# A two-layer decoder trunk on one core: window values as a difference, input weights kept split, early products by operand half, and running sums on GpSimd

## The chip, the core and the metric

The kernel runs on one core of a Trainium2 chip. The core has TensorE for matrix products (PE in the profile, with its weight loads as PEld), VectorE (DVE), ScalarE (ACT), GpSimd (POOL) and SyncE (SP), which issues most of the DMAs. The metric is the device time of one execution in microseconds. Before the change three runs took 1911.7 us (median), 1904.19 us and 2302.37 us.

## The reference

The input is x of 1024 positions by 1024 channels, in 32-bit floats. There are two layers, and each has two sub-layers, with an RMS norm before and after each, and with shift, scale and gate made from a vector c by a product with `ada_w`.

```python
h = rms_norm(x, g_pre_mix[l]) * (1.0 + scale_m) + shift_m
proj = h @ w_in[l] + b_in[l]                       # 1024 -> 512 q, 128 k, 128 v, 512 u
q, k = partial_rotary(q), partial_rotary(k)        # first 16 of 64 dims of each head
attn_out = sliding_window_attention_with_sinks(q, k, v, sinks[l])   # 8 heads, 2 kv heads, window 128
pool_out = causal_pool_mixer(u, pool_w[l], pool_scale[l])           # means over 2, 4, 8, 16 positions
mix = concat([attn_out, pool_out]) @ w_out[l]
x = x + gate_m * rms_norm(mix, g_post_mix[l])
h = rms_norm(x, g_pre_ffn[l]) * (1.0 + scale_f) + shift_f
f = (silu(h @ w_gate[l]) * (h @ w_up[l])) @ w_down[l]               # 1024 -> 2816 -> 1024
x = x + gate_f * rms_norm(f, g_post_ffn[l])
```

With blocks of 128 positions, a query at place i of its block sees the keys at places j > i of the block before, and the keys at j <= i of its own block. In the first block there are only its own keys. The softmax also has one sink logit per head. The pooling mixer takes, for each of four groups of 128 channels, the mean over the last 2, 4, 8 or 16 positions, subtracts the token itself, and maps the group by a 128x128 matrix.

## The kernel before

Every large product is made from operands that are split in two: `hi` is the operand rounded to TensorE's 32-bit matmul format, `lo` is the rest, and `mm3` (L268 in the profile) adds three products, hi by hi, hi by lo and lo by hi. `split` makes the two parts: an ACT copy (L220) and a DVE subtraction (L221). So each weight tile that comes from memory costs one DMA, one ACT and one DVE instruction before TensorE can use it. `weight` loads and splits one tile (512 columns); `one_ahead` hands it out and asks for the next one, so that one tile is prepared ahead.

The positions are worked on in two halves (h = 0 and 1) of 512, each in four tiles t of 128. In a layer the mixing stage comes first, and then the channel-mixing stage, which is a dense run of products. The mixing stage goes as follows.

- `q_pass`, `kv_pass` and `u_pass` project a half: for each of 8 slices k of the channels (4 double slices in `kv_pass`) they take a weight tile and make 12 products of 512 columns (256 in `kv_pass`). Each weight of `w_in` is thus loaded and split twice in a layer, once for each half.
- `attention(h)` gives 8 groups, one for each tile t and each kv head n. A group makes transposed keys and queries, scores (`att_scores`, one 128x128 score tile a head, in which the places j > i hold the scores with the block before and the others those with its own block), the softmax, transposed probabilities (`att_probs`), and the product with the values (`att_values`, into the bank `pv`). Before the change `att_probs` made two masked copies by four GpSimd selects: `here`, with j <= i (L1048), and then `seen` masked in place to j > i (L1053). `here` met the block's own values and `seen` those of the block before.
- `pool_mix(h)` gives four steps, one for each window width. A width w needs log2(w) running sums over 527 columns or fewer (L1145, on DVE), a scaled subtraction (L1149), a split, and one `mm3`, which is issued one step late.
- `mix_out(h)` multiplies the concatenated result by `w_out` in `natural_proj`: two halves nh of the output columns, each in four banks of PSUM, first with the pooled channels (4 slices), then with the attention's. Ahead of the first attention slice it calls `finish_off(last)`, which issues whatever of the half's attention is left.
- While half 1 is mixed, half 0 goes on: `post_norm` (L695, sums of squares L596, a chain of short instructions L327 to L334), `normalise` (L636 on DVE, L638 on ACT), eight transposed pieces (`pre_norm_piece`, ACT L649), and then `up_firsts`: early products of the channel-mixing stage for three column pairs p and two halves kh of the depth. kh = 0 needs pieces 0 to 3, and kh = 1 needs pieces 4 to 7.

TensorE's order in this part is written by hand. `weave(main, *sides)` walks through the dense work (`main`), and each side chain becomes due after a number of columns has been issued. A gap is given in STEPs of 12 x 512 columns, that is 12 products. `LEADS` holds the gaps inside an attention group, `attention`'s last argument is the gap between groups, and the numbers in `yield` are those of the other chains. The other engines' orders follow from the order of the program and a scheduler. Each engine works through its own queue in order, and so does SP with the DMAs.

## Time and profile before

| what | value |
|---|---|
| median of 3 runs | 1911.7 us |
| the profiled execution's own time | 1908.17 us |
| its span, first to last instruction | 1906.5 us |
| TensorE busy | 1852.5 us, 97% of the span |
| VectorE busy | 1522.5 us, 80% |
| ScalarE busy | 938.1 us, 49% |
| GpSimd busy | 128.9 us, 7% |
| mean granted TensorE clock | 0.993 |
| DMA | 341.81 MB, mean 179 GB/s |

The mixing stage of layer 0 lies between about 30 and 275 us of the span, and that of layer 1 between about 955 and 1215 us. In between, and after, lie the channel-mixing stages. A TensorE instruction's duration in the profile is longer than the time from its start to the next start, since products overlap; the time to the next start is what a product costs. A stretch in which an engine waits is shown in square brackets with what ended it. PEclk is the share of full clock that TensorE was granted.

### The profile page before, as it was taken

How to read it: one execution, taken by the hardware profiler on the slowest of the kernel's cores; microseconds unless marked ns; L12 is line 12 of the kernel's file. 1: busy time of each engine (PE TensorE's matmuls, PEld its weight loads, DVE VectorE, ACT ScalarE, POOL GpSimd, SP SyncE). 2: the span in 40 equal slices, each digit the busy share in tenths (PEclk: the TensorE clock that was granted, in tenths of full speed). 3: DMA queues.
4: the chain of work that ended last, by engine and by line, in shares of the span. 5: the costliest groups of instructions: out<-in, count | busy, mean ns of one | idle time of the engine just before them, and what ended most of it. 6: DMA issues, size and time to landing. Idle time of an engine off the chain costs nothing. (4 is left out here: it accounts for less than half of the span.)

```text
span 1906.5 us, 25287 instructions
## 1 busy us (share of the span) xinstructions
PE 1852.5 (97%) x8662; PEld 1519.9 (80%) x8662; DVE 1522.5 (80%) x2507; ACT 938.1 (49%) x1775; POOL 128.9 (7%) x226
## 2 busy tenths in 40 slices
PE   7999989999999999999999998999999999999998
PEld 5877778888878788888887876788888887888886
DVE  7898876678898888788868988756878888867687
ACT  4775686663222223445558757855622222234452
POOL 0022122000000000000001312210000000000000
PEclk9999999999999999999999999999999999999999
DMA  9346554555555665944553573446654565574343
GB/s 333 124 135 182 187 160 144 188 172 188 199 176 190 209 204 167 325 150 149 172 180 93 166 228 122 139 149 204 216 190 148 199 214 195 193 254 159 116 138 116
DMA packets 229536, 341.81 MB, mean 179 GB/s; under 512 B 17016, under 2 KB 126472, under 8 KB 229408
## 3 DMA queue, kind: packets, MB, share of 16 engines
q1 hardware_dynamic: 228800, 338.10, 54.0%
q10 hardware_dynamic: 576, 2.10, 0.3%
q8 instruction: 68, 1.11, 0.2%
q14 instruction: 60, 0.49, 0.1%
q0 software_dynamic: 32, 0.00, 0.0%
HBM read 267.25 MB, written 72.89 MB: 178 GB/s over the span
## 5 line engine op out<-in xcount | busy, mean ns | idle before, releaser
L220 ACT ACTIVATE hi<-raw 128x1024 fp32r<-128x1024 f32 (+1 forms) x388 | 332.9, 869 | 404.1 <-PE acc L268 255.4
L221 DVE TENSOR_TENSOR lo<-raw,hi 128x1024 fp32r<-128x1024 f32 (+1 forms) x388 | 385.1, 999 | 117.8 <-ACT hi L220 113.3
L268 PE MATMUL acc<-t,hi 128*128 128x512 f32 x1408 | 432.3, 390 | 2.4 <-ACT hi L220 2.3
L268 PEld LDWEIGHTS acc<-t,hi 128*128 128x128 f32 x1408 | 263.8, 188 | 58.8 <-ACT hi L220 4.8
L268 PE MATMUL acc<-hT,hi 128*128 128x512 f32 x960 | 304.9, 399 | 4.7 <-ACT hi L220 3.0
L268 PE MATMUL acc<-t,lo 128*128 128x512 f32 x704 | 272.3, 390 | 1.0 <-DVE lo L221 1.0
L268 PEld LDWEIGHTS acc<-hT,hi 128*128 128x128 f32 x960 | 175.1, 190 | 38.9 <-ACT hi L220 3.9
L268 PE MATMUL acc<-bh,hi 128*128 128x512 f32 x520 | 203.0, 390 | 0.0
L268 PE MATMUL acc<-bh,lo 128*128 128x512 f32 x520 | 202.6, 390 | 0.0
L268 PE MATMUL acc<-hT,lo 128*128 128x512 f32 x480 | 189.2, 394 | 0.0
L1313 DVE TENSOR_TENSOR fn<-acc,fn 128x512 f32<-128x512 f32 x220 | 150.4, 684 | 38.8 <-PE acc L268 38.6
L268 PEld LDWEIGHTS acc<-t,lo 128*128 128x128 f32 x704 | 132.2, 188 | 30.4 <-DVE lo L221 3.0
L268 PE MATMUL acc<-ph,hi 128*128 128x512 f32 x328 | 126.6, 390 | 0.0
L268 PE MATMUL acc<-hi,hT 128*128 128x512 f32 (+1 forms) x448 | 123.4, 348 | 1.0 <-ACT hT L220 1.0
L1240 ACT ACTIVATE fn<-fn 128x512 f32<-128x512 f32 x44 | 27.8, 633 | 181.2 <-DVE fn L1313 181.2
L268 PEld LDWEIGHTS acc<-bh,lo 128*128 128x128 f32 x520 | 97.7, 188 | 20.3
L268 PEld LDWEIGHTS acc<-bh,hi 128*128 128x128 f32 x520 | 97.7, 188 | 20.0
L268 PE MATMUL acc<-b,hi 128*128 128x512 f32 x352 | 108.4, 389 | 0.0
L268 PEld LDWEIGHTS acc<-hT,lo 128*128 128x128 f32 x480 | 91.0, 190 | 20.5 <-DVE lo L221 0.9
L268 PE MATMUL acc<-hi 128*128 128x512 f32 x256 | 102.8, 402 | 3.9 <-ACT hi L220 2.8
L268 PE MATMUL acc<-lo,hi 128*128 128x512 f32 x256 | 101.3, 396 | 0.1
L220 ACT ACTIVATE bh<-two_b 128x512 fp32r<-128x512 f32 x100 | 62.3, 623 | 71.4 <-PE acc L268 70.7
(304 smaller groups left out, 3238.8 us busy)
## 6 DMA issues: line engine op xcount, KB each, us to landing
raw<-in_w_gate_dram SPq DMA_DIRECT2D x44, 512.0 KB
raw<-in_w_up_dram SPq DMA_DIRECT2D x44, 512.0 KB
raw<-in_w_in_dram SPq DMA_DIRECT2D x80, 256.0 KB
cfb<-in_ada_w_dram SPq DMA_DIRECT2D x80, 256.0 KB
raw<-keeps SPq DMA_DIRECT2D x40, 512.0 KB
keeps<-fn SPq DMA_DIRECT2D x66, 256.0 KB
ar<-in_ada_w_dram SPq DMA_DIRECT2D x64, 256.0 KB
two_b<-in_w_down_dram SPq DMA_DIRECT2D x30, 512.0 KB
```

The costliest lines, as they stand in the source:

```text
L220: a = nc.scalar.activation(hi, src, AF.Copy)
L221: v = nc.vector.tensor_sub(lo, src, hi.bitcast(F32))
L268: return nc.tensor.matmul(dst, lhs, rhs, start=start, stop=stop)
L1240: nc.scalar.activation(g, g, AF.Silu)
L1313: nc.vector.tensor_add(halves_of(dst)[m], bank, halves_of(src)[m])
```

## The change

Four things are changed, together with numbers that set TensorE's order.

1. **Values with a difference.** `seen` is no longer masked. All probabilities of a tile, masked by nothing, meet the values of the block before, and the copy `here` (j <= i) meets the difference of the block's own values and those of the block before. The sum is the same. Two of the four selects of a group go, and for the first block both. The difference is made by GpSimd (`tensor_sub`, 128x128, once a tile) and split by ACT and DVE into new tiles `dz`. The product with the unmasked probabilities comes first, and the one with `here` after a gap of its own.
2. **Weights stored split.** `weight_once` writes the two parts of a tile to memory (two DMAs of 256 KB) when it is first made, and loads both by one DMA of 512 KB when it is next needed. This is done for all weights `u` and, in layer 1, also for `q` and `kv`: 28 tiles.
3. **Early products in another order.** For the first three column pairs `up_firsts` makes kh = 0 of all pairs first, and then kh = 1 of all; pieces 4 to 7 are so needed 16 groups of three products later.
4. **Running sums on GpSimd** in `pool_mix` (now L1152).

Besides, `natural_proj` of half 1 takes two of its four banks for nh = 1 from another pool of banks, the score rows are 192 columns apart instead of 129, and `one_ahead` can prepare two tiles ahead (for `u` of half 1). The core of the diff:

```diff
+    def weight_once(key, *srcs):
+        if key in parted:
+            both = part("lo", 1024)
+            nc.sync.dma_start(both.bitcast(F32), parted.pop(key))
+            return both[:, 0:512], both[:, 512:1024]
+        hi, lo = weight(*srcs)
+        if key[0] == "u" or key[-1] == "1":
+            parted[key] = both = dr.tile([P, 1024], F32, tag=key, name="parted", bufs=1)
+            for i, src in enumerate((hi, lo)):
+                nc.sync.dma_start(both[:, i * 512 : (i + 1) * 512], src.bitcast(F32))
+        return hi, lo
...
-            banks = [acc_bank() for _ in range(NT)]
+            spare = 2 if nh and free else 0
+            banks = [msc_bank() for _ in range(spare)] + [acc_bank() for _ in range(spare, NT)]
...
-        for v in views:
-            nc.gpsimd.affine_select(
-                out=v, in_=v, pattern=[[0, GRP], [-1, P]], compare_op=ALU.is_gt,
-                fill=0.0, base=0, channel_multiplier=1,
-            )
...
+            if n == 0:
+                if blk:
+                    nc.gpsimd.tensor_sub(step, qkvs[t][:, QK:QKV], attn["raw"])
+                attn["raw"] = qkvs[t][:, QK:QKV]
...
-            yield LEADS[4]
-            att_values(blk, n, probs, cat, t)
+                used = [attn["v"], att_vals("dz", step)] if blk else []
+                attn["v"] = att_vals("vz", qkvs[t][:, QK:QKV])
+                attn["vals", blk] = used or [attn["v"]]
+            parts = list(zip(attn["vals", blk], probs))
+            for i, (vals, prob) in enumerate(parts):
+                yield LEADS[4 + i]
+                att_values(n, vals, prob, n + i == 0, n == NKV - 1 and i == len(parts) - 1, cat, t)
-    LEADS = (0.8, 0.8, 0.25, 3.2, 2.2)
+    LEADS = (0.9, 0.85, 0.21, 2.72, 1.2, 0.94)
...
-                nc.vector.tensor_add(nxt[:, lo:n], cur[:, lo:n], cur[:, lo - width : n - width])
+                nc.gpsimd.tensor_add(nxt[:, lo:n], cur[:, lo:n], cur[:, lo - width : n - width])
...
-            yield 2.0 if h else 3.0
+            yield 1.7 if h else 2.82
...
-        jobs = [(p, kh) for p in pairs for kh in range(2)]
+        jobs = [(p, kh) for kh in range(2) for p in pairs] if room else [(p, kh) for p in pairs for kh in range(2)]
...
-        att = attention(0, qkvs[0], par["sink"], cats[0][0], 0.5, 3.8)
+        att = attention(0, qkvs[0], par["sink"], cats[0][0], 0.47, 3.23)
...
-        att = attention(1, qkvs[1], par["sink"], cats[1][0], 14.0, 4.2)
+        att = attention(1, qkvs[1], par["sink"], cats[1][0], 14.0, 3.95)
...
-                yield 0.5
+                yield GAPS[k // HK]
...
-        ask1 = one_ahead(all_rows(u_rows, l))
+        ask1 = one_ahead(all_rows(u_rows, l), 2)
...
-                if i == 2 * HK - 1:
+                if i == 2 * HK * FIRST[0] - 1:
```

Three places show what moves. The first is TensorE's queue in layer 0, where the last attention group of half 0 ends inside `mix_out(0)`. `msc<-ident,sb` are the transposes of the probabilities, `pv<-pth,vz` and `pv<-pth,dz` the products with values and with their difference, `acc<-...` those of `mix_out`; `uT` and `pt` are the low parts of its left operand, `pt` from the first attention slice on. Before:

```order
L273 MATMUL msc<-ident,sb 128x128 x4
L268 MATMUL acc<-hi 128x512
L268 MATMUL acc<-lo,hi 128x512
L268 MATMUL acc<-hi,uT 128x512
L268 MATMUL acc<-hi 128x512
L268 MATMUL acc<-lo,hi 128x512
L268 MATMUL acc<-hi,uT 128x512
L268 MATMUL acc<-hi 128x512
L268 MATMUL acc<-lo,hi 128x512
L268 MATMUL acc<-hi,uT 128x512
L268 MATMUL pv<-pth,vz 128x512 x6
L268 MATMUL acc<-hi 128x512
```

With the change the last group's transposes stand in front of `mix_out(0)`, 31 rows ahead of its last product:

```order
L285 MATMUL acc<-hi 128x512
L285 MATMUL acc<-lo,hi 128x512
L285 MATMUL acc<-hi,uT 128x512
L285 MATMUL pv<-pth,dz 128x512 x3
L285 MATMUL acc<-hi 128x512
L285 MATMUL acc<-lo,hi 128x512
L285 MATMUL acc<-hi,uT 128x512
```

The last value products stood 9 products behind the transposes, right ahead of the first attention slice; now they stand further from the transposes, and products of pooled slices (`uT`) follow them.

The second place is POOL's queue in layer 0 while half 1 is pooled. `pth<-pth` are the selects on the probabilities, `pt<-uT` the first and `pt<-pt` the further running sums of a width, `sb<-qkv` the difference of the values. Before:

```order
L1048 AFFINE_SELECT pth<-pth 128x512 x2
L1053 AFFINE_SELECT pth<-pth 128x512 x2
L931 CAST vz<-vz_zero 128x64 x2
L1098 COPY sb<-sk 128x4
L1048 AFFINE_SELECT pth<-pth 128x512 x2
```

And with the change:

```order
L1059 AFFINE_SELECT pth<-pth 128x512 x2
L948 CAST vz<-picks 128x64 x2
L1152 TENSOR_TENSOR pt<-pt 128x525
L1152 TENSOR_TENSOR pt<-pt 128x521
L948 CAST dz<-picks 128x64 x2
L1152 TENSOR_TENSOR pt<-uT 128x527
L1152 TENSOR_TENSOR pt<-pt 128x525
L1098 TENSOR_TENSOR sb<-qkv 128x128
L1152 TENSOR_TENSOR pt<-pt 128x521
L1101 COPY sb<-sk 128x4
L1152 TENSOR_TENSOR pt<-pt 128x513
L1059 AFFINE_SELECT pth<-pth 128x512 x2
```

Six running sums (the last two of width 8 and all four of width 16) now stand between the selects of two neighbouring attention groups.

The third place is SP's queue in layer 0 at the start of `u_pass` of half 0. `raw<-in_w_in_dram` are loads of weight tiles, `cfa<-in_ada_w_dram` loads for the gate, `parted` the stores of split weights. Before:

```order
L233 DMA raw<-in_w_in_dram 128x512 x2
L551 DMA cfa<-in_ada_w_dram 128x512 x4
L233 DMA raw<-in_w_in_dram 128x512 x3
L522 DMA ar<-in_ada_b_dram 1x512
L523 DMA ar<-in_g_post_mix_dram 1x512
```

And with the change:

```order
L236 DMA raw<-in_w_in_dram 128x512 x2
L568 DMA cfa<-in_ada_w_dram 128x512 x4
L253 DMA parted<-hi 128x512
L253 DMA parted<-lo 128x512
L253 DMA parted<-hi 128x512
L253 DMA parted<-lo 128x512
L236 DMA raw<-in_w_in_dram 128x512 x3
L539 DMA ar<-in_ada_b_dram 1x512
L540 DMA ar<-in_g_post_mix_dram 1x512
```

The loads of the next three tiles now stand behind the stores of two tiles, and a store waits until its tile is split.

More of the change, by code (lines that the diff above doesn't have):

```diff
@@ L97, in hybrid_decoder_kernel @@
     dr = ctx.enter_context(tc.tile_pool(name="dr", bufs=1, space=DRAM))
-    SMALL = dict(junk=1, st=9, rs=8, ss=4, halo=8, rows=1, cols=2, colp=4, sk=2)
+    const.tile([P, 32], F32, name="fill")
+    ident_r = const.tile([P, P], F32R, name="ident")
+    const.tile([P, 56], F32, name="fill2")
+    SMALL = dict(junk=1, st=9, rs=8, ss=4, halo=4, cols=2, colp=4, sk=2)
     SHARED = dict(hT=8, fn=4, raw=2, hi=3, lo=3, sa=2, sb=2, ar=2, ada=1, ph=3, G=1)
     REGIONS = dict(
-        mix=dict(cfa=2, cfb=2, qkv=5, bqkv=1, uT=4, pt=2, vz=5, qT=1, pth=4, pwh=1, pwl=1),
+        mix=dict(cfa=2, cfb=2, qkv=5, bqkv=1, uT=4, pt=2, vz=4, dz=2, qT=1, pth=4, pwh=1, pwl=1),
         up=dict(t2=8, t1=8, t3=8, b22=8, t4=8),
@@ L243, in after, with one_ahead @@
         )
-    def one_ahead(makers):
+    def one_ahead(makers, ahead=1):
         makers = iter(makers)
-        held = [next(makers)()]
+        held = [make() for _, make in zip(range(ahead), makers)]
         def ask():
-            now_ = held.pop()
             for make in makers:
@@ L254, in ask @@
                 break
-            return now_
+            return held.pop(0)
         return ask
@@ L757, in finish, with natural_proj @@
             nc.sync.dma_start(out[0, h * T + rows.start : h * T + rows.stop, cs], fn[t][:, cs])
-    def natural_proj(fn, left, wsrc, ss, G, last):
+    def natural_proj(fn, left, wsrc, ss, G, last, free):
         K = len(left)
@@ L803, in drain @@
             pass
-    vz_zero = const.tile([P, HD], F32, name="vz_zero")
-    nc.vector.memset(vz_zero, 0.0)
     halos = {}
@@ L1160, in pool_mix, with mix_out @@
             late = (g, hi, lo_)
[L1161 removed]
+            yield 1.7 if h else 2.82
         mapped(*late)
[L1164 removed]
+    def mix_out(l, cats, G, last, free=False):
         order = [*range(GRP, KD), *range(GRP)]
@@ L1179, in mix_out @@
         ss = t_("ss", [P, 8])
-        return fn, ss, natural_proj(fn, left, wsrc, ss, G, last)
+        return fn, ss, natural_proj(fn, left, wsrc, ss, G, last, free)
     HK = KD // 2
@@ L1255, in operand @@
             return hi, lo
-        nxt = operand(*jobs[0])
+        nxt, xs_ = operand(*jobs[0]), []
         yield
@@ L1630, in gate_flow @@
             one, two = ada_gate(l, 0)
-            yield from ada_flow([one], [cats[0][1][:, i, :] for i in range(4)], 1.8)
+            yield from ada_flow([one], [cats[0][1][:, i, :] for i in range(4)], 2.25)
             while 1 not in cats:
                 yield 0.5
-            yield from ada_flow([two], [cats[1][1][:, i, :] for i in range(4)], 1.8)
+            yield from ada_flow([two], [cats[1][1][:, i, :] for i in range(4)], 1.91)
         gate = Chain(gate_flow())
-        att = attention(0, qkvs[0], par["sink"], cats[0][0], 0.5, 3.8)
+        att = attention(0, qkvs[0], par["sink"], cats[0][0], 0.47, 3.23)
         def dense():
```

89 lines of the change are left out of this document (39 added, 50 removed).

## The prediction

> **What bounds the kernel now.** I read the page first, then busy time by stretches, then who TensorE waited for in the stretches where it idles, and last the order of instructions around those waits. The page says that TensorE is the bound:
>
> ```profile
> span 1906.5 us, 25287 instructions
> ...
> PE 1852.5 (97%) x8662; PEld 1519.9 (80%) x8662; DVE 1522.5 (80%) x2507; ACT 938.1 (49%) x1775; POOL 128.9 (7%) x226
> ```
>
> The change leaves the number of products as it is: a group of attention has six value products before and after, the early products only change places. So what can be won is TensorE's idle time and its slow clock. The view by stretches shows where these lie. After the stretch and its length come busy us and instruction counts of PE, PEld, DVE, ACT and POOL, then the granted clock, DMA share and GB/s.
>
> ```profile
> 30.00:160.00 130.00, 127.39 (x749) 108.59 (x749) 114.91 (x245) 93.81 (x231) 24.86 (x49) 1.00 0.51 165
> 160.00:176.00 16.00, 13.25 (x48) 9.20 (x47) 14.65 (x27) 6.57 (x16) 5.45 (x7) 0.91 0.67 208
> 176.00:225.00 49.00, 47.92 (x221) 37.28 (x220) 41.92 (x88) 30.64 (x80) 3.19 (x6) 1.00 0.65 207
> 225.00:275.00 50.00, 42.02 (x222) 33.79 (x221) 39.11 (x77) 42.73 (x95) 15.17 (x22) 0.97 0.49 158
> 275.00:955.00 680.00, 677.36 (x3050) 558.87 (x3050) 543.32 (x765) 292.47 (x458) 14.60 (x21) 1.00 0.57 187
> 955.00:1098.00 143.00, 140.58 (x791) 119.79 (x790) 119.40 (x253) 97.68 (x240) 25.76 (x52) 1.00 0.47 147
> 1098.00:1112.00 14.00, 11.53 (x40) 7.73 (x40) 12.39 (x22) 4.73 (x9) 5.13 (x7) 0.88 0.65 194
> 1112.00:1160.00 48.00, 46.81 (x218) 36.30 (x217) 41.17 (x86) 30.08 (x78) 3.18 (x6) 1.00 0.63 205
> 1160.00:1215.00 55.00, 47.51 (x234) 38.39 (x233) 40.54 (x79) 44.89 (x100) 15.73 (x26) 0.91 0.44 148
> 1215.00:1300.00 85.00, 84.47 (x393) 69.38 (x392) 52.47 (x93) 51.86 (x111) 12.77 (x17) 1.00 0.42 134
> 1300.00:1850.00 550.00, 548.73 (x2434) 453.03 (x2433) 440.09 (x607) 213.81 (x301) 0.00 (x0) 1.00 0.56 186
> ```
>
> The two long dense stretches idle 2.6 us of 680 and 1.3 us of 550, and the change barely touches them. The nine others are the mixing stages. Length less busy PE gives 2.6, 2.8, 1.1, 8.0, 2.4, 2.5, 1.2, 7.5 and 0.5 us, 28.5 us together. The clock (1 less PEclk, times length) adds 1.4, 1.5, 1.7 and 5.0 us in the four stretches below 1.00, 9.6 us. So about 38 us can be won at most, 2.0% of the span. Three parts: the running of attention beside the projections (30 to 160, 955 to 1098; call it A, 5.0 us), the end of the first half's attention (160 to 176, 1098 to 1112; B, 5.2 us idle and 3.1 of clock), and the second half's start (225 to 275, 1160 to 1215; C, 15.5 us idle and 6.5 of clock). The rest is 2.8 us. PE's waits in B of layer 0 and in C of layer 0 (engine, line, waited for: total us, times, longest):
>
> ```profile
> PE acc L268 <- ACT hi L220: 1.4, 1, 1.4
> PE pv L268 <- POOL pth L1048: 0.9, 2, 0.6
> PE pv L268 <- POOL pth L1053: 0.5, 2, 0.3
> ...
> PE msc L273 <- DVE fn L636: 2.2, 2, 2.0
> PE msc L273 <- DVE hi L970: 2.0, 1, 2.0
> PE acc L268 <- ACT hi L220: 1.5, 1, 1.5
> PE msc L273 <- ACT raw L649: 1.2, 1, 1.2
> PE msc L268 <- ACT qT L982: 0.9, 1, 0.9
> ```
>
> One product's price, 225.03 / 991 = 0.227 us, and so 2.72 us for a STEP of 12, comes from the chain of waits:
>
> ```profile
> 1611.47 225.03 PE acc L268 x991
> ```
>
> **The change part by part.** *End of attention (B).* The four selects of the last group stand between transposes and value products, and nothing covers them, since only 9 products (2.0 us) lie between; then `mix_out` waits 1.4 us for the cast of the finished output. With the change the groups start every 3.23 STEPs instead of 3.8: 7 x 0.57 x 2.72 = 10.9 us earlier for the last of eight, and the leads inside a group are 7.25 - 6.82 = 0.43 STEP shorter, 1.2 us more. The queue in front of this text shows the same: the last products leave before the attention slices come. If the earlier place holds, all of B goes, 8.3 us. What would uncover it again is a group that runs 5 us late.
>
> *Stored weights.* Each of 28 second uses loses a cast and a subtraction:
>
> ```profile
> L220 ACT ACTIVATE hi<-raw 128x512 fp32r<-128x512 f32 x167 | 103.5, 628 | 122.4 <-PE acc L268 83.7 <-issue 22.0 <-DMA raw<-in_w_in_dram 12.6
> L221 DVE TENSOR_TENSOR lo<-raw,hi 128x512 fp32r<-128x512 f32 x167 | 118.3, 716 | 51.9 <-ACT hi L220 47.6 <-DMA raw<-in_w_gate_dram 2.1 <-DMA raw<-keeps 1.8
> ```
>
> That is 17.6 us of ACT and 20.0 us of DVE. Only the 16 `u` tiles lie in C. There the wait for ACT's cast (L220, 1.5 us a layer, 3.0 for two) goes, since that cast is no longer made. The price lies in half 0: SP's stores wait for the split of a tile prepared one step ahead, and three loads are queued behind. Three loads issued from 40.03 on fed a cast at 43.92:
>
> ```profile
> 40.03 1.76 SPq L233 DMA_DIRECT2D raw<-in_w_in_dram  x3
> ...
> 43.92 0.62 ACT L220 ACTIVATE hi<-raw 128x512 fp32r<-128x512 f32 x1
> ```
>
> so the path from one tile's split to the next batch's is 0.63 + 0.72 + 3.9 + 0.63 + 0.72 = 6.6 us, and with 0.3 us for a store's issue 6.9 us, against two steps of about 3.2 us (12 products and the transposes of a piece): 0.5 us late, twice a pass, in two layers: 2 us. Bounds: nothing, if the tiles are split earlier; 2.5 us each time, 10 us, if each cast and subtraction waits behind a wide one (1.06 and 1.22 us in the rows below).
>
> *Early products by half.* Pieces 4 to 7 were forced one behind the other; PE then waited for L649 (1.2 us, in layer 1 0.8). Now they have 16 groups of three products, 16 x 0.68 = 10.9 us, and gaps of 1.06 STEP. I count all 2.0 us. The silu of three pairs also moves behind all kh = 0 jobs; nothing on PE's path is credited for that.
>
> *Running sums.* DVE loses 16, 12, 8 and 4 sums of about 0.7 us, 29 us in all. What a sum costs on GpSimd no row shows. The nearest are its selects, which read one operand:
>
> ```profile
> L1053 POOL TENSOR_SCALAR_AFFINE_SELECT pth<-pth 128x512 fp32r<-128x512 f32 x56 | 47.1, 864 | 0.0
> L1048 POOL TENSOR_SCALAR_AFFINE_SELECT pth<-pth 128x512 fp32r<-128x512 f32 x56 | 41.4, 739 | 43.2 <-ACT pth L220 34.9 <-DVE pth L221 6.3 <-DVE rs L332 1.4
> L1098 POOL COPY sb<-sk 128x4 f32<-128x4 f32 x32 | 15.6, 486 | 283.6 <-PE msc L273 203.8 <-DVE cfb L636 28.8 <-ACT hi L969 16.7
> L931 POOL CAST vz<-vz_zero 128x64 fp32r<-128x64 f32 x32 | 9.9, 329 | 666.4 <-DVE fn L636 627.4 <-PE pv L268 39.1
> ...
> L934 DVE TENSOR_TENSOR vz<-qkv,vz 128x128 fp32r<-128x128 f32 x16 | 4.8, 298 | 1.5 <-PE pv L268 1.5
> L1145 DVE TENSOR_TENSOR pt<-uT 128x527 f32<-128x527 f32 x16 | 12.0, 748 | 3.7 <-ACT uT L901 2.6 <-POOL pth L1053 0.6
> ```
>
> A sum reads two operands: between 0.74 us (one select) and 1.73 us (two of the slower). I take 1.3 us. The Trainium skill (GPSIMD Engine Reference, Performance versus the Vector engine) gives 4497 ns for an add of 2048 columns, by which 527 would take an estimated 1.16 us; it also says that such work belongs on VectorE, which speaks against this part of the change. No run here shows it yet.
>
> In the tightest place six sums stand between the selects of two groups: 6 x 1.3 = 7.8 us, two selects 1.7, and two copies, four casts and a difference about 2.7 us, 12.2 us against a group's period of 3.95 x 2.72 = 10.7 us. From the transposes to the masked product there are 2.14 STEPs, 5.8 us, of which a cast, a subtraction and two selects take 3.0; the 2.8 us left cover the 1.5 us of delay. In half 0 it is four sums, 8.7 us with the rest, against 8.8. I count 1 us for all of it. Selects removed (L1053 and the first blocks') give POOL back 53 us, about what 40 sums cost.
>
> *What DVE's relief is worth.* In C two waits are on DVE: L636, at the end of a chain of short instructions that had eight weight splits around it, and L970, which had two running sums in the 5 us ahead of it, but also a wide subtraction and ACT's exponentials. I take half of each, 2.1 us a layer, 4.2. In A the relief meets groups that are packed 15% closer; I count nothing. The values' difference adds 14 casts and 14 subtractions of 0.3 us, covered by products.
>
> *Clock.* The low clock in C stands where waits of 2 us follow each other. Of 7.8 us of waits a layer 4.6 go; I take 60% of the 6.5 us, 3.9.
>
> *Sum.* 8.3 + 3.0 + 2.0 + 4.2 + 3.9 = 21.4 us gained, 2 + 1 lost, 18.4 net. The profiled execution took 1908.2 us, 1.7 over its span, and lies 0.2% under the median of 1911.7. That gives 1889.8; I say 1890.
>
> **The rivals.** *The port.* A DVE subtraction beside a select is held up: this multiply-add took 1.12 us and this subtraction 1.11, against 0.745 (mean of the group in the next fence) and 0.72 alone.
>
> ```profile
> 167.76 1.12 DVE L564 SCALAR_TENSOR_TENSOR ada<-cfb,c_act,ada 128x512 f32<-128x512 f32 x1
> 168.29 1.75 POOL L1053 TENSOR_SCALAR_AFFINE_SELECT pth<-pth 128x512 fp32r<-128x512 f32 x2
> ...
> 169.47 1.11 DVE L221 TENSOR_TENSOR lo<-raw,hi 128x512 fp32r<-128x512 f32 x1
> ...
> L351 DVE SCALAR_TENSOR_TENSOR ada<-ar,c_act,ada 128x512 f32<-128x512 f32 x56 | 41.7, 745 | 3.2 <-DMA ar<-in_ada_w_dram 3.0
> ```
>
> If each sum holds DVE for its whole 1.3 us, 52 us are taken where 29 were given, most of them in C. Then the 4.2 us stay and most of the clock's 3.9: 1890 + 8 = 1898. The Trainium skill (SBUF — State Buffer, Who interferes with whom) states such a rule: a VectorE instruction with two SBUF inputs and a GpSimd instruction that reads SBUF exclude each other for a whole instruction. The rows above agree that there is a hold, but of 0.4 us. Chance 0.25.
>
> *Stores hold the loads.* The 10 us bound instead of 2, since SP's queue is strictly in order: 1898, and 2 us of clock: 1900. Chance 0.15.
>
> *Everything goes.* If DVE's relief ends A and C as well, 38 less 2 us: 1872. Against it speaks that ACT is busy 42.7 of 50 us in C, more than DVE (39.1). Chance 0.08.
>
> *POOL too late, slower than before.* A sum on POOL waits until DVE's wide subtraction is done, and then reads twice:
>
> ```profile
> L221 DVE TENSOR_TENSOR lo<-raw,hi 128x1024 fp32r<-128x1024 f32 x219 | 266.1, 1220 | 66.0 <-ACT hi L220 65.7
> L220 ACT ACTIVATE hi<-raw 128x1024 fp32r<-128x1024 f32 x219 | 228.9, 1057 | 279.5 <-PE acc L268 169.5 <-DVE raw L1334 41.2 <-issue 30.7
> ```
>
> 1.22 + 1.73 = 2.95 us. The selects behind six sums are then 6 x 2.95 + 4.4 - 10.7 - 2.8 = 8.6 us late for PE in half 1, and behind four 3.7 us in half 0: 25 us in two layers, and four slow-clock stretches of some 1.7 us (as in B), 7. That is 1890 + 32 - 1 = 1921. It turns the gain into a loss from about 2.3 us a sum on. POOL's low load (25 of 130 us busy in A, 15 of 50 in C) speaks against it. Chance 0.07.
>
> **How the numbers follow.** My forecast has 0.45; its own range is 1884 to 1896 (half and all of the L636 and L970 waits, stores at 0 or 5 us). Leaving out the last rival (0.07) and the lower part of "everything goes", the range is 1876 to 1905. 2% is about what a measurement of this kernel can tell from no change. Faster by over 2% means under 1873, which needs nearly all of the 38 us: half of 0.08, 0.04. Slower by over 2% means over 1950, beyond the worst rival: 0.02. The rest, 0.94, is within 2%.
>
> **What would show it.** Right: no PE wait for POOL's selects and for ACT's cast around 160 and 1100 us; in the stretch after, no wait for L220 and L649, shorter ones for DVE; a sum of 1.2 to 1.4 us; DVE some 45 us less busy. Wrong: waits of `pv<-pth,dz` for selects (POOL late), PE waits for ACT's weight casts in `u_pass` of half 0 (stores), DVE subtractions of 1.5 us and more beside sums (port), or waits in A that have grown because the groups are packed closer.

## The result, and the profile after

The changed kernel took 1882.8 us (median of four runs, 1881.56 to 1884.28) beside 1907.95 us before. That median is over four runs, of which one was in a slow state (2302.37 us); the ratio leaves that run out. The ratio is 0.9875, with a 95% interval of 0.9845 to 0.9905: faster by 1.25%, some 24 us, and less than the 2% that the prediction took as the least that can be told. The forecast was 1890 us, with a range of 1876 to 1905 and 0.94 on "within 2%". So the total came out near the forecast. The terms that it was made of did not.

The profiled execution took 1884.28 us. Its page, with TensorE still the bound:

```profile
span 1882.5 us, 25362 instructions
...
PE 1838.8 (98%) x8662; PEld 1516.4 (81%) x8662; DVE 1492.7 (79%) x2452; ACT 920.6 (49%) x1757; POOL 145.1 (8%) x244
```

The views by stretches of before and of after, cut at the same places of the program. For each layer they show the running of attention beside the projections (A), then all of `mix_out(0)` (the end of attention, B, with the rest of that product), and then the second half from its start to the end of its attention (C). Columns as in the prediction. Before:

```profile
67.00:151.00 84.00, 81.39 (x476) 67.91 (x475) 74.64 (x156) 67.06 (x171) 19.46 (x35) 1.00 0.41 129
151.00:211.00 60.00, 56.74 (x249) 43.56 (x249) 50.99 (x93) 32.02 (x77) 9.51 (x15) 0.97 0.67 208
211.00:310.00 99.00, 90.45 (x466) 73.89 (x465) 77.52 (x160) 80.70 (x191) 28.66 (x42) 0.98 0.46 150
...
1004.00:1087.00 83.00, 80.58 (x475) 67.92 (x474) 73.60 (x152) 66.33 (x169) 19.86 (x35) 1.00 0.42 131
1087.00:1147.00 60.00, 56.92 (x250) 43.60 (x249) 50.98 (x93) 32.45 (x78) 9.18 (x15) 0.97 0.67 210
1147.00:1248.00 101.00, 92.94 (x463) 75.97 (x462) 77.08 (x159) 80.30 (x190) 27.78 (x42) 0.95 0.44 147
```

After:

```profile
68.00:160.00 92.00, 87.73 (x508) 73.78 (x507) 79.78 (x165) 71.49 (x191) 34.69 (x49) 0.98 0.50 163
160.00:208.00 48.00, 47.59 (x219) 38.56 (x218) 43.20 (x77) 26.96 (x57) 3.15 (x8) 1.00 0.78 250
208.00:297.00 89.00, 87.00 (x462) 71.72 (x461) 69.92 (x146) 74.97 (x188) 33.00 (x48) 1.00 0.51 177
...
990.00:1086.00 96.00, 88.86 (x505) 73.92 (x504) 72.67 (x152) 66.75 (x180) 30.09 (x48) 0.96 0.64 203
1086.00:1134.00 48.00, 47.60 (x221) 38.67 (x220) 41.52 (x73) 25.20 (x54) 2.37 (x8) 1.00 0.75 233
1134.00:1224.00 90.00, 87.92 (x466) 72.47 (x465) 70.42 (x148) 75.86 (x190) 31.97 (x48) 1.00 0.54 180
```

B and C are nearly full now, at full clock. A has become worse: it idles 4.3 and 7.1 us, and it has lost clock. A itself has more in it than before, since more of attention is done there. So I measured each stretch by what it costs above its products. From the starts of all products in the trace, a product of 512 columns takes 0.2265 us to the next start where nothing hinders it, and one of 256 takes 0.1175. For a 128x128 transpose I took 0.062; most take 0.08 to 0.11, so some 3 us of the excess of each A and each C (104 to 128 transposes) are no loss, before and after alike. "Excess" is the length of a stretch less that time of its products:

| excess, us | layer 0 before | after | layer 1 before | after |
|---|---|---|---|---|
| A, attention beside the projections | 10.9 | 14.2 | 10.2 | 18.4 |
| B, `mix_out(0)` | 8.7 | 1.1 | 8.5 | 1.1 |
| C, second half's start and attention | 17.7 | 8.7 | 20.3 | 8.8 |
| `mix_out(1)` | 0.8 | 0.1 | 0.8 | 0.1 |

B gained 15.0 us, C 20.5 and `mix_out(1)` 1.4, together 36.9. A lost 11.5. The difference, 25.4, is the gain of the span (24.0) and 1.4 us lost elsewhere. The parts of the table that stood at low clock were 8.2 us before (B and C) and are 4.2 now (all in A).

What TensorE waits for in A of layer 1 after (engine, line, waited for: us, times, longest). A load of a stored tile stands first:

```profile
PE acc L285 <- DMA lo<-parted: 3.1, 2, 2.4
PE msc L285 <- ACT qT L999: 2.2, 3, 1.0
PE msc L290 <- ACT sa L979: 1.3, 1, 1.3
```

SyncE's queue in the same stretch waits with these loads (L247) until a slot for the tile is free, 8.3 us once:

```profile
SPq L247 <- PE acc L285: 13.8, 3, 8.3
```

And the running sums on GpSimd, by form:

```profile
L1152 POOL TENSOR_TENSOR pt<-uT 128x527 f32<-128x527 f32 x16 | 19.7, 1234 | 13.4 <-DVE pt L1161 9.1 <-ACT uT L918 2.7 <-DVE pt L1156 1.6
...
L1152 POOL TENSOR_TENSOR pt<-pt 128x525 f32<-128x525 f32 x12 | 13.2, 1102 | 26.7 <-DVE lo L224 22.6 <-DVE st L1037 4.0
L1152 POOL TENSOR_TENSOR pt<-pt 128x521 f32<-128x521 f32 x8 | 11.2, 1406 | 0.4
...
L1152 POOL TENSOR_TENSOR pt<-pt 128x513 f32<-128x513 f32 x4 | 5.2, 1302 | 0.1
```

They make 49.3 us for 40, 1.23 us each. I had taken 1.3. VectorE waits for them 11 times (its L1156, the scaled subtraction), 14.7 us together.

### The profile page after: what moved, and what is told of

It is laid out like the page before. It is cut to its first block, busy times and chain, and to the rows that moved or that the text cites. A ratio compares the mean times of both kernels' runs of the same rounds, so it can differ in the third digit from the quotient of the medians.

```text
span 1882.5 us, 25362 instructions
## 1 busy us (share of the span) xinstructions
PE 1838.8 (98%) x8662; PEld 1516.4 (81%) x8662; DVE 1492.7 (79%) x2452; ACT 920.6 (49%) x1757; POOL 145.1 (8%) x244
## 4 chain that ended last, share of the span: by engine, by line
PE 77%; DVE 11%; DMA 4%; ACT 4%; issue 2%; POOL 1%; SPq 1%; DVEq 0%; ACTq 0%; POOLq 0%
PE acc L285 71%; PE msc L285 2%; PE msc L290 2%; DVE lo L224 2%; DMA raw<-in_w_up_dram 2%; PE pv L285 2%; ACT hi L223 1%; POOL pt L1152 1%; DMA ar<-x 1%; DMA raw<-in_w_in_dram 1%; DVE ada L581 1%; DVE hT L224 1%; DVE fn L1322 1%; ACT sb L1034 0%; DVE st L1026 0%
## 5 line engine op out<-in xcount | busy, mean ns | idle before, releaser
L223 ACT ACTIVATE hi<-raw 128x1024 fp32r<-128x1024 f32 (+2 forms) x360 | 315.4, 888 | 389.6 <-PE acc L285 246.4
L224 DVE TENSOR_TENSOR lo<-raw,hi 128x1024 fp32r<-128x1024 f32 (+2 forms) x360 | 364.1, 1019 | 118.0 <-ACT hi L223 114.7
L285 PE MATMUL acc<-hT,hi 128*128 128x512 f32 x832 | 260.3, 394 | 0.0
L285 PE MATMUL acc<-hT,lo 128*128 128x512 f32 x608 | 213.1, 393 | 0.5 <-DVE lo L224 0.4
L1322 DVE TENSOR_TENSOR fn<-acc,fn 128x512 f32<-128x512 f32 x220 | 150.6, 685 | 36.9 <-PE acc L285 36.6
L285 PEld LDWEIGHTS acc<-hT,hi 128*128 128x128 f32 x832 | 151.7, 188 | 28.1
L285 PEld LDWEIGHTS acc<-hT,lo 128*128 128x128 f32 x608 | 112.4, 188 | 25.4 <-DVE lo L224 1.3
L285 PE MATMUL acc<-lo,hT 128*128 128x512 f32 (+1 forms) x352 | 96.1, 349 | 3.6 <-DMA lo<-parted 3.1
L285 PE MATMUL acc<-hi,hT 128*128 128x512 f32 (+1 forms) x320 | 89.9, 355 | 1.0 <-ACT hT L223 1.0
L285 PE MATMUL acc<-hi 128*128 128x512 f32 x224 | 87.6, 391 | 0.8 <-DVE fn L806 0.8
```

Of the source, the lines that this page charges most:

```text
L223: a = nc.scalar.activation(hi, src, AF.Copy)
L224: v = nc.vector.tensor_sub(lo, src, hi.bitcast(F32))
L285: return nc.tensor.matmul(dst, lhs, rhs, start=start, stop=stop)
L1322: nc.vector.tensor_add(halves_of(dst)[m], bank, halves_of(src)[m])
```

## The experiments

Every median below stands beside a median of the kernel before of 1907.9 to 1908.9 us on the same chip. Where two runs below are set against each other, these medians differ by up to 1 us. The first four runs each undo one part of the changed kernel.

**Running sums back on VectorE.**

```diff
-                nc.gpsimd.tensor_add(nxt[:, lo:n], cur[:, lo:n], cur[:, lo - width : n - width])
+                nc.vector.tensor_add(nxt[:, lo:n], cur[:, lo:n], cur[:, lo - width : n - width])
```

> The changed kernel with one part undone: the running sums of the pooling mixer are made by VectorE again. Theory of the prediction: the sums on GpSimd relieve VectorE by 29 us and cost PE about 1 us; without them the DVE waits of the second half's start come back in part, 1885 to 1888 us. Port rival: a sum of 1.23 us on GpSimd holds VectorE nearly as long as the 0.7 us it saves, and the new waits in the attention beside the projections (1.7 us for ACT L1039 and 1.2 for ACT L979 in layer 0, 1.3 for L979 in layer 1) come from sums that are late; without them 1877 to 1880 us.

Measured: 1867.5 us (1866.8 to 1868.7), ratio 0.979 (0.9774 to 0.9807). That is 15.3 us faster than the changed kernel. So this part of the change costs time, and "DVE's relief" has the wrong sign. The stretches after this edit, to be set beside those of after:

```profile
67.00:154.00 87.00, 84.95 (x505) 72.22 (x504) 79.69 (x172) 71.12 (x190) 23.21 (x39) 1.00 0.53 172
...
202.00:289.00 87.00, 86.64 (x463) 72.14 (x462) 72.70 (x157) 75.15 (x190) 20.78 (x38) 1.00 0.53 182
...
982.00:1073.00 91.00, 85.56 (x503) 71.89 (x502) 75.72 (x163) 66.33 (x180) 19.57 (x38) 1.00 0.67 215
```

The excess is 9.6 and 13.6 us in A (14.2 and 18.4 with the sums on GpSimd) and 6.3 and 6.4 in C (8.7 and 8.8). Nothing stands at low clock any more. How a sum reaches TensorE is seen in the changed kernel's timeline (start, us, engine, line, operation; in brackets the wait and its releaser):

```profile
123.85 1.06 POOL L1152 TENSOR_TENSOR pt<-uT 128x527 f32<-128x527 f32 x1 [2.46 <-DVE pt L1161]
123.87 1.07 DVE L1162 TENSOR_TENSOR pt<-pt,uT 128x16 f32<-128x16 f32 x1
124.03 0.19 ACT L1034 ACTIVATION_READ_ACCUMULATOR sb<-sb,st 128x1 f32 x1
...
124.87 0.74 DVE L581 SCALAR_TENSOR_TENSOR ada<-cfb,c_act,ada 128x512 f32<-128x512 f32 x1
...
125.53 0.16 DVE L1037 RECIPROCAL st<-st 128x4 f32<-128x4 f32 x1
...
126.52 1.11 PE L290 MATMUL msc<-ident,sb 128*128 128x128 f32 x4 [1.68 <-ACT sb L1039]
126.63 1.55 DVE L581 SCALAR_TENSOR_TENSOR ada<-cfb,c_act,ada 128x512 f32<-128x512 f32 x1
```

and at the same place with the sums on VectorE:

```profile
120.60 0.19 ACT L1034 ACTIVATION_READ_ACCUMULATOR sb<-sb,st 128x1 f32 x1
...
120.97 0.17 DVE L1037 RECIPROCAL st<-st 128x4 f32<-128x4 f32 x1
...
121.88 0.81 PE L290 MATMUL msc<-ident,sb 128*128 128x128 f32 x4
...
122.13 0.16 DVE L1162 TENSOR_TENSOR pt<-pt,uT 128x16 f32<-128x16 f32 x1
```

A subtraction over 16 columns (L1162), which takes 0.16 us alone, starts 0.02 us after a sum on GpSimd and takes 1.07 us, as long as the sum. Behind it in VectorE's queue waits the softmax's reciprocal (L1037): it comes 1.31 us after the exponentials' end (124.22) instead of 0.18 (120.79). About 0.9 us of this is the held subtraction. The rest is L581, which the scheduler put ahead here and behind there. TensorE waits 1.68 us for it. L581, 0.75 us alone, takes 1.55 at the next sum.

The Trainium skill (SBUF — State Buffer, Who interferes with whom) says that a VectorE instruction with two SBUF inputs and a GpSimd instruction that reads SBUF exclude each other for a whole instruction, and that one with at most one SBUF input does not contend, unless it runs in a mode that uses both ports. These rows agree with the first; the split that reads PSUM and SBUF (`pth<-msc,pth`) agrees with the second: it takes 683 ns in the changed kernel and 682 ns with the sums on VectorE.

**No stored weights** (and the old distance of one tile ahead).

```diff
-        if key[0] == "u" or key[-1] == "1":
+        if False:
...
-        ask1 = one_ahead(all_rows(u_rows, l), 2)
+        ask1 = one_ahead(all_rows(u_rows, l))
```

> The changed kernel with one part undone: no weight is stored split, each is loaded and split again at its second use, and the u weights of half 1 are prepared one ahead, as before. Theory of the prediction: the wait for ACT's weight casts in the second half's start (3.0 us for two layers) returns and its clock with it, and the stores' price goes (predicted 2 us, and 3.1 us of waits for stored kv tiles seen in layer 1): 1881 to 1886 us, a draw. Rival: the stores are what made the attention beside the projections worse by 11.5 us, so without them 1873 to 1877 us. Other rival: DVE and ACT casts in that part are what counts, 1888 or more.

Measured: 1896.95 us (1894.2 to 1898.9), 14.1 us over the changed kernel. C loses 4.7 us in layer 0 and 4.6 in layer 1 (excess 13.4 in both), and A of layer 0 loses 2.7 (16.9). A of layer 1 gains 1.8 (16.6), since there the loads of the stored `kv` tiles are gone. So the stores do not hold up half 0; A of layer 0, where I had put their price, is better with them. What costs seems to be the loads in layer 1, which the last run tests. The run undoes two things at once, and how the 14.1 us divide between the stored weights and the second tile ahead is open.

**Four selects** (values without the difference, all else as changed).

```diff
+        for v in seen:
+            nc.gpsimd.affine_select(
...
+                pattern=[[0, GRP], [-1, P]], compare_op=ALU.is_gt, fill=0.0, base=0, channel_multiplier=1,
             )
         return [seen, here]
...
-                used = [attn["v"], att_vals("dz", step)] if blk else []
+                used = [attn["v"]] if blk else []
                 attn["v"] = att_vals("vz", qkvs[t][:, QK:QKV])
-                attn["vals", blk] = used or [attn["v"]]
+                attn["vals", blk] = used + [attn["v"]]
```

> The changed kernel with one part undone: both copies of the probabilities are masked again (four selects a group, two more for the first block) and meet the values of the two blocks, no difference is made. Order and leads of the products stay. Theory of the prediction: the end of the first half's attention gains by the earlier place of the groups, not by the selects, so its waits stay away; POOL has 53 us more, its queue is late for some products: 1884 to 1888 us. Rival: fewer selects are what made the change fast, 1890 us or more.

Measured: 1922.9 us (1918.1 to 1927.4), 40.1 us over the changed kernel and 0.8% over the kernel before (ratio 1.008, 1.0055 to 1.0105). TensorE waits for the second selects, most of all:

```profile
PE pv L285 <- POOL pth L1069: 28.8, 27, 3.8
```

B stays empty all the same: `mix_out(0)` has an excess of 1.1 us in layer 0 and 1.2 in layer 1. So it is not the selects that emptied B, but the place of the groups.

This run holds more than two selects a group, though. The product that TensorE issues first, 1.2 STEPs behind the transposes, meets `seen`, which GpSimd masks last (L1069); before the change the first product came 2.2 STEPs behind them and met `here`, which is masked first. Had `seen` been masked first, it would have been ready earlier by an estimated 1.6 us (two selects of 0.81 us, the mean of L1064 in this run), and the 27 waits are 1.07 us on average. So by this estimate much of the 28.8 us comes from the order of the selects, and what two selects more cost in a good order was not tried.

**Early products pair by pair.**

```diff
-        jobs = [(p, kh) for kh in range(2) for p in pairs] if room else [(p, kh) for p in pairs for kh in range(2)]
+        jobs = [(p, kh) for p in pairs for kh in range(2)]
...
-                if i == 2 * HK * FIRST[0] - 1:
+                if i == 2 * HK - 1:
```

> The changed kernel with one part undone: the early products go pair by pair again, so that pieces 4 to 7 are needed after 7 groups of products instead of 23. Theory of the prediction: the wait for L649 comes back, 2.0 us in two layers, and some slow clock: 1885 to 1888 us. Rival: this order is what emptied the second half's start (20.5 us less lost than before, of which I had foreseen 13.1): 1890 to 1895 us.

Measured: 1894.1 us (1891.4 to 1895.9), 11.3 us over the changed kernel. The excess of C is 13.1 and 13.6 us instead of 8.7 and 8.8, so the order is worth much more than the 2.0 us that I had read from two waits for L649.

The next four ask what makes the sums and the selects cost so much, and what the pace is worth.

**The sums on VectorE, and useless adds on GpSimd beside them.**

```diff
-UW = 576
+UW = 528
...
+    waste = const.tile([P, HALO + T], BF16, name="waste")
...
-                nc.gpsimd.tensor_add(nxt[:, lo:n], cur[:, lo:n], cur[:, lo - width : n - width])
+                nc.vector.tensor_add(nxt[:, lo:n], cur[:, lo:n], cur[:, lo - width : n - width])
+                nc.gpsimd.tensor_add(waste[:, lo:n], u[:, lo:n], u[:, lo - width : n - width])
```

> The kernel with the sums on VectorE (1867.5 us), in which GpSimd makes a further add of the same size beside each of the 40 running sums, into a tile that nobody reads (40 adds are made for nothing, in bfloat16, and the tiles of the pooling mixer are 528 instead of 576 columns wide). Nothing waits for these adds except a buffer that they read. If the 15 us that the move to GpSimd costs come from VectorE being held while GpSimd reads, they are here as well: about 1882 us, or up to 1890 since VectorE keeps its own sums too. If they come from the way round through GpSimd, that is from a sum that takes 1.23 instead of 0.70 us and from two engines waiting for each other, nothing of it is here: 1868 to 1870 us. In between, the shares can be read off.

Measured: 1899.5 us (1898.0 to 1901.7), 32.0 us over the run with the sums on VectorE alone, though nothing needs these adds. So the longer way through GpSimd is not needed to explain the loss: adds that run beside VectorE's work are enough. VectorE is 26.5 us busier with them (1527.7 us against 1501.2, over the same 2492 instructions), and in this run no wait of TensorE, VectorE or ScalarE for GpSimd is listed, so it is not a late result of GpSimd that costs the time. The timeline in C of layer 0, VectorE and GpSimd:

```profile
247.87 9.62 POOL L1154 TENSOR_TENSOR waste<-uT 128x527 bf16<-128x527 f32 x7
...
250.34 1.02 DVE L1028 TENSOR_SCALAR st<-st 128x4 f32<-128x4 f32 x1
251.27 0.68 DVE L224 TENSOR_TENSOR pwl<-raw,pwh 128x512 fp32r<-128x512 f32 x1
251.87 1.55 DVE L224 TENSOR_TENSOR lo<-pt,uT 128x512 fp32r<-128x512 f32 x1
253.45 1.45 DVE L1153 TENSOR_TENSOR pt<-pt 128x525 f32<-128x525 f32 x1
254.82 0.17 DVE L1038 RECIPROCAL st<-st 128x4 f32<-128x4 f32 x1
```

Seven adds run back to back for 9.6 us. In this time VectorE's chain from L1028 to the reciprocal takes 4.5 us, and TensorE then waits 5.0 us for the probabilities:

```profile
PE msc L290 <- DVE sb L1044: 5.0, 1, 5.0
```

**The sums on VectorE, and four selects.** The edits of the first and the third run together.

> The changed kernel with the sums on VectorE and with the four selects back (values without the difference). With the sums on GpSimd the selects cost 40 us (1922.9 against 1882.8), and there TensorE waited 28.8 us for them. If the cost is that of selects queued behind running sums on GpSimd, most of it goes with the sums: 1875 to 1885 us. If the selects are too long for the shorter leads by themselves, it stays: 1900 to 1908 us.

Measured: 1894.2 us (1892.8 to 1900.4). It lies between the two expectations. The two selects more cost 26.6 us here and 40.1 with the sums on GpSimd, so 13.5 us come from sharing GpSimd with the sums, and 26.6 belong to the selects within these leads and in the order told above. TensorE's waits for them shrink to less than half, and there are still 21:

```profile
PE pv L285 <- POOL pth L1069: 12.8, 21, 1.8
```

**Running sums on GpSimd, alone.** The kernel before, with this one edit.

```diff
-                nc.vector.tensor_add(nxt[:, lo:n], cur[:, lo:n], cur[:, lo - width : n - width])
+                nc.gpsimd.tensor_add(nxt[:, lo:n], cur[:, lo:n], cur[:, lo - width : n - width])
```

> The kernel before with its running sums on GpSimd and nothing else. If moving them costs the same anywhere, 15 us more than before: 1924 us. If what they cost depends on the selects that share GpSimd's queue (112 of them here, 56 in the changed kernel), more: by the difference between the two runs with four selects, which the other experiment gives, 1935 to 1950 us, with TensorE waiting for selects. If there is room because this kernel's groups start further apart, less: 1910 to 1915 us.

Measured: 1919.2 us (1915.5 to 1925.0), ratio 1.0067 (1.0046 to 1.0089): 11.3 us lost. The move costs something of the same size in both kernels, and twice as many selects in the same queue do not make it worse: behind one wait for a load at the kernel's start, TensorE's list has VectorE and ScalarE in its first places and no select. Of the loss 7.2 us lie in A (excess 14.6 and 13.7 against 10.9 and 10.2); in C one layer loses 1.1 and the other gains 1.5. The rest lies outside these stretches and was not followed.

**The old pace.**

```diff
-        att = attention(0, qkvs[0], par["sink"], cats[0][0], 0.47, 3.23)
+        att = attention(0, qkvs[0], par["sink"], cats[0][0], 0.47, 3.8)
...
-        att = attention(1, qkvs[1], par["sink"], cats[1][0], 14.0, 3.95)
+        att = attention(1, qkvs[1], par["sink"], cats[1][0], 14.0, 4.2)
```

> The changed kernel with the old gaps between attention groups (3.8 and 4.2 STEPs instead of 3.23 and 3.95). If it is the pace that emptied the end of the first half's attention (four selects or two, the end was empty in all runs so far), some 4 us idle come back there in each layer, and the running of attention beside the projections gets back up to half of its 11 us: 1883 to 1890 us. If the pace is worth the whole of what that part gained (7.6 us a layer), 1893 to 1898 us. If it only moved the loss from one part to the other, no difference, 1881 to 1884 us.

Measured: 1909.3 us (1906.1 to 1914.6), ratio 1.0009 (0.9999 to 1.0019). All three expectations were too low: two numbers undo the whole gain. The end of the first half's attention gets 5.4 us a layer back, as the first of them said, but C also loses 10.2 and 9.8 us (excess 18.9 and 18.6), which none of them had.

The last four separate what was left.

**Fills instead of adds.** As the run with useless adds, but GpSimd writes zeros to the spare tile three times where that run made an add.

```diff
-                nc.gpsimd.tensor_add(waste[:, lo:n], u[:, lo:n], u[:, lo - width : n - width])
+                [nc.gpsimd.memset(waste[:, lo:n], 0.0) for _ in range(3)]
```

> The kernel with the sums on VectorE and the narrower tiles of the run with useless adds (1899.5 us), in which GpSimd fills the spare tile three times with zeros where that run made an add: GpSimd is about as long busy at the same places of its queue, but reads no operand (the fills are made for nothing). If the useless adds cost 32 us because GpSimd reads from SBUF while VectorE reads two operands there, nothing of that is left: 1867 to 1872 us, and VectorE as busy as without any adds (1501 us, against 1528). If what cost the time was the place that they took in GpSimd's queue, ahead of selects and copies, or the narrower tiles, it is here too: 1890 to 1900 us.

Measured: 1877.6 us (1874.4 to 1878.3). Of the 32.0 us, 21.9 are gone. But the fills did not run where the adds had run. The adds and then the fills (durations in ns, then the first and the last start in us):

```profile
L1154 POOL TENSOR_TENSOR waste<-uT x40: 1058/1392/1632, 93.5 to 1190.6; 128x527 bf16<-128x527 f32 x16, 128x525 bf16<-128x525 f32 x12, 128x521 bf16<-128x521 f32 x8, 128x513 bf16<-128x513 f32 x4
```

```profile
L1154 POOL MEMSET waste<- x120: 525/536/952, 3.6 to 88.3; 128x527 bf16 x48, 128x525 bf16 x36, 128x521 bf16 x24, 128x513 bf16 x12
```

A fill waits for nothing, so all 120 ran before 89 us, those that belong to layer 1 too, ahead of all pooling. "At the same places of its queue" is therefore not what was run: in C, in layer 1 and in most of A of layer 0 this is a run with neither adds nor fills, on the narrower tiles. It shows again what the adds cost. It does not show what other work of GpSimd would cost in their place.

VectorE's busy time in the two runs, with the same 2492 instructions (first the adds, then the fills):

```profile
PE 1844.0 (97%) x8662; PEld 1521.0 (80%) x8662; DVE 1527.7 (80%) x2492; ACT 921.8 (49%) x1757; POOL 153.0 (8%) x244
```

```profile
PE 1833.6 (98%) x8662; PEld 1513.0 (81%) x8662; DVE 1505.0 (80%) x2492; ACT 919.1 (49%) x1757; POOL 163.9 (9%) x324
```

In A and C the excess is 10.9, 13.7, 7.1 and 6.5 us here (9.6, 13.6, 6.3, 6.4 with neither), and 16.8, 20.0, 13.5 and 13.8 with adds. The instructions of the fence above, now with nothing beside them, take their usual time:

```profile
245.11 0.16 DVE L1028 TENSOR_SCALAR st<-st 128x4 f32<-128x4 f32 x1
...
245.78 0.68 DVE L224 TENSOR_TENSOR lo<-pt,uT 128x512 fp32r<-128x512 f32 x1
246.49 0.70 DVE L1153 TENSOR_TENSOR pt<-pt 128x525 f32<-128x525 f32 x1
247.11 0.17 DVE L1038 RECIPROCAL st<-st 128x4 f32<-128x4 f32 x1
```

What fills do to VectorE can be read where they ran. The 60 TENSOR_TENSOR instructions that overlap one kept their time: 28.8 us together, as with the medians of the same forms in the run with neither; among them the weight splits (`lo<-raw,hi`, 512 columns) at 686 ns against 685. The 35 TENSOR_SCALAR instructions, which have one tile and a scalar as inputs, did not: 17.9 us together instead of 8.6. One of them, with fills and in the run with neither:

```profile
26.68 0.82 DVE L437 TENSOR_SCALAR ar<-cfb,c_act 128x512 f32<-128x512 f32 x1
```

```profile
23.84 0.48 DVE L437 TENSOR_SCALAR ar<-cfb,c_act 128x512 f32<-128x512 f32 x1
```

10 us over the run with neither remain, of which 3.2 lie before A, where the fills ran, and 2.3 in A and C; whether the narrower tiles make part of them was not tried.

**Half 1's old pace alone** (4.2; half 0 keeps 3.23).

> The changed kernel with the old gap between the attention groups of half 1 alone (4.2 instead of 3.95 STEPs); half 0 keeps 3.23. With both gaps old the time is 1909.3, 26.5 us more, of which 20 lie in the second half's start and 11 in the end of the first half's attention, less 4 in layer 0's running beside the projections. If each gap acts in its own part, the second half's start loses its 10 us a layer here, and the end of the first half stays empty: 1900 to 1904 us. If the second half's start depends on half 0's gap, through the later start of all that follows: 1883 to 1887 us.

Measured: 1898.4 us (1893.8 to 1900.7), 15.6 us over the changed kernel. B stays empty (1.1 us) and C loses 4.4 and 5.6 us, `mix_out(1)` 1.4 in each layer. So half 1's gap acts in its own part, as the first expectation has it, but only about half of what C lost with both gaps old is here. The other half needs half 0's old gap, by itself or together with this one; half 0's alone was not run.

**The new pace alone.** The kernel before, with 3.23 and 3.95.

> The kernel before with the two new gaps between attention groups (3.23 and 3.95 STEPs) and nothing else. If the pace alone empties the end of the first half's attention, with four selects and the old, longer gaps inside a group: 15 us less there, of which the running beside the projections takes 5 to 8 back, and the second half's start is as before: 1898 to 1903 us. If the closer groups need the two selects less that the change makes, TensorE waits for GpSimd's selects instead: 1908 to 1920 us.

Measured: 1903.4 us (1899.0 to 1910.8), ratio 0.998 (0.9965 to 0.9994): 4.6 us won by the medians, just above the first expectation. The pace by itself empties B, with four selects (second row, to be set beside 151 to 211 us of before), and A pays for most of it (first row):

```profile
67.00:162.00 95.00, 87.55 (x502) 74.68 (x500) 82.32 (x168) 70.56 (x186) 28.44 (x43) 0.96 0.40 123
162.00:210.00 48.00, 47.91 (x221) 38.96 (x221) 44.43 (x77) 27.93 (x58) 5.26 (x8) 1.00 0.83 261
```

B gains 8.0 and 7.8 us, A loses 7.3 and 6.0.

**The sums on VectorE, and only the `u` weights stored.**

```diff
-        if key[0] == "u" or key[-1] == "1":
+        if key[0] == "u":
```

> The changed kernel with the sums on VectorE (1867.5 us) and with only the u weights stored, not q and kv of layer 1. If the loads of the stored kv tiles cost what they seem to (2.7 us of waits in layer 1, and there 4 us more idle time beside the projections than in layer 0), and the q and kv splits that come back are covered: 1862 to 1865 us. If the splits that come back cost as much as the loads: 1867 to 1869 us.

Measured: 1864.2 us (1861.6 to 1865.4), ratio 0.9771 (0.9753 to 0.9789). This is the fastest version that was run: 2.3% under the kernel before and 18.6 us under the changed one. Both edits take something out of the change. A of layer 1 now has an excess of 9.4 us instead of 13.6, and no wait for a stored tile. TensorE's waits there are only these:

```profile
PE acc L285 <- DVE lo L224: 1.2, 2, 1.0
PE msc L285 <- ACT qT L999: 0.7, 1, 0.7
```

## Why the prediction was right or wrong

The time was 7 us under the forecast, well inside the range and just under the forecast's own narrower range (1884 to 1896). It was right as a sum of errors with different signs: the stretches that gained gave 36.9 us where the sum had 21.4, and the one that lost took 11.5 where the sum had 3. That the total fits is luck, and the range was held for other reasons than the prediction gave.

**What DVE's relief is worth: wrong in sign.** This is the step that failed. I took 4.2 us gained, and 1 us lost for late sums; the runs showed 15.3 us lost here and 11.3 alone. The instruction's length was right (1.23 us for 1.3). Its effect on VectorE's load was not: I had expected some 45 us less in all, and it fell by 29.8 (1522.5 to 1492.7). Against the run with the sums on VectorE the load is only 8.5 us less (1501.2), though 40 sums of about 0.7 us, some 29 us, are gone. The difference is time in which VectorE's other instructions were held, 20.5 us if every form is compared with its mean in that run. In the changed kernel VectorE also waits for the sums that it used to make itself (14.7 us); how the loss divides between this and the holds was not separated.

**The port rival: right in kind, too small.** I gave it 0.25 and 8 us. What misled me was its size: a hold of 0.4 us beside a select. The sums held short instructions for their whole length. The rival's own sum was off as well: it had 52 us of holds cost 8 us, and 20.5 us of holds went with a loss of 15.3. My price was also put into C, where I had seen the waits on VectorE; of the 15 us, 9.4 are in A (4.6 and 4.8) and 4.8 in C. That adds on GpSimd make VectorE longer busy, and the kernel slower, is shown by the run with useless adds. That it is their reading that holds a two-input instruction rests on the TENSOR_TENSORs that kept their time beside fills, early in the kernel; fills at the places of the adds were not run. That a held instruction delays TensorE through the softmax was seen in the timeline at one place in A and at one in C, and counted nowhere. The Trainium skill (GPSIMD Engine Reference, Performance versus the Vector engine), by which such work belongs on VectorE, would have given the right sign here; the 1.16 us estimated from its figure stand beside 1.23 measured.

**A: counted as nothing, lost 11.5 us.** 9.4 of it are the sums. In layer 1 loads of stored `kv` tiles cost more: with them gone, A of layer 1 falls from 13.6 to 9.4 us and is then as good as layer 0's (10.2). I had named waits grown by closer groups as a sign against me, and with the pace alone A does lose 13.3 us in two layers; without the sums, and with only `u` stored, it has no more excess than before. What in the change gives that back was not separated.

**End of attention: right, and larger.** I said that all of B goes, 8.3 us, by the earlier place of the groups. All of it went, 15.0 us: the idle time before and behind the two stretches that I had cut out belonged to it. That the place does it, and not the selects, is shown by the run with four selects and by the pace alone. But the place has a price that I counted as nothing: with the pace alone A takes back 13.3 of B's 15.8 us.

**Stored weights: mis-sized.** 3.0 us gained and 2 lost in my sum; undoing them, with the second tile ahead, costs 14.1. The price that I gave to the stores is not seen. The price that exists, the loads that wait for a slot, was not in the sum, and "stores hold the loads" (0.15) did not happen.

**Early products: mis-sized.** 2.0 us in my sum, 11.3 when undone.

**Clock: mis-sized, and A's share missed.** The excess at low clock fell by 4.0 us, from 8.2 to 4.2. My 3.9 were for C alone, and B's 3.1 stood in the 8.3, so my sum had 7.0 and the likeness of 3.9 and 4.0 is chance. All of it went in C (some 5.4, four stretches of 3.4 us at half clock) and in B (some 2.9, two stretches), and A got 4.2, which I had not foreseen.

**"POOL too late": did not happen.** A sum stayed far from 2.3 us, and TensorE's list has 0.3 us of waits for a select in C. With four selects, in the order told above, TensorE did wait for them: 28.8 us with the sums on GpSimd and 12.8 with the sums on VectorE.

**The parts do not add up.** Undone one at a time, the stored weights, the selects, the order and the pace cost 14.1, 40.1, 11.3 and 26.5 us, 92 us together, where the four and the sums' loss make some 24. (The 40.1 us also hold the order of the selects.) Alone on the kernel before, the pace was worth 4.6. Each undoing brings back about half of what C had won, or all of it (excess of C in layer 0 of 13.4, 17.6, 13.1 and 18.9 against 8.7). So C needs all of them as they were undone here, and no share of C's 20.5 us can be given to one of them. I had priced each part by the waits that it removes; that prices the first part that is taken away from a schedule, not the last that is put in. How the stored weights, the difference and the order of the early products act alone on the kernel before was not tried, and neither was what the banks from the other pool, the wider score rows and the smaller changes of other gaps are worth.

## What to carry to other kernels

Before work moves from VectorE to GpSimd, count VectorE's two-input SBUF instructions and its TENSOR_SCALARs that will run beside it, and look for short ones that a chain such as the softmax stands behind: here one was held as long as the moved instruction lasted, and a lower busy time of VectorE says nothing about that. When an experiment puts other work in the place of some work, look in its trace where that work ran: the fills that were to stand in for adds ran up to a millisecond earlier. When a change has several parts and new gaps, run it without each part: here it was faster without one of its four, and faster still with half of another. A loss in a stage to which the sum gave nothing (A, 11.5 us) is found only when whole stages are compared, not the waits that one meant to remove.

## What was unexpected of the hardware

- A VectorE subtraction over 16 columns took 1.07 us instead of 0.16 because a sum on GpSimd had started 0.02 us before it, and 53.0 us of useless adds on GpSimd made VectorE 26.5 us busier over the same 2492 instructions. Beside fills on GpSimd (120 of 0.55 us), 60 TENSOR_TENSOR instructions of VectorE kept their time, and 35 TENSOR_SCALARs took 17.9 us instead of 8.6.
- An instruction over four columns with one tile as input (`st<-st`, a TENSOR_SCALAR) was held too: 1.02 us beside the adds, 0.16 beside none, and 298 against 190 ns as the mean of all 32. I had looked only at instructions with two operands. The Trainium skill (VectorE: DVE Perf Modes, Mode 2×_2P) has a mode for such an instruction that uses both read ports; the rows agree with that, and no run here shows the mode itself.
